# Winograd convolution on one core: the first input loads split by rows over two DMA queues, and zero-matmuls placed on both sides of the weight transposes

## The chip, the cores and the metric

The kernel runs on one core of one Trainium2 chip. The metric is the device time of one execution in microseconds (us); the time before is the median of three runs, 126.69 us (126.35 to 126.71). A core has five engines: TensorE (PE in the profile), VectorE (DVE), ScalarE (ACT), GpSimd (POOL) and SyncE (SP). SyncE, ScalarE and GpSimd can issue transfers; each of the three has a queue of its own, and the packets of all queues are carried by the same 16 DMA engines.

## The reference

A 3 x 3 convolution with padding 1, 16 images of 64 channels and 64 x 64 pixels, 128 output channels, all in float32:

```python
def setup_inputs():
    batch, c_in, h, w, c_out = 16, 64, 64, 64, 128
    ...
    x_pad = np.pad(x, ((0, 0), (0, 0), (1, 1), (1, 1)), mode='constant')
    ...
                        output[b, co] += weight[co, ci, kh, kw] * x_pad[b, ci, kh:kh+h, kw:kw+w]
```

The input has 16.8 MB, the output 33.6 MB, the weights 0.29 MB.

## The kernel before, in words

**Tiling.** Two images are one pair: their 2 x 64 channels fill the 128 partitions, one partition holding one channel's 64 x 64 pixels (16 KB). There are eight pairs (`p`), and a pair's 64 output rows are made in four blocks (`blk`) of 16 rows. A matmul uses the 64 partitions of one image and 512 columns (8 rows of 64); the matmuls of the two images stand in turn. Vertically the kernel computes two output rows from shared products (a small Winograd scheme): with `ss`, the sum of each even row and the odd row below it, it forms U = G1 * ss, then A from the odd rows (weights G2 - G1, and G0 on the row above) and B from the even rows (weights G0 - G1, and G2 on the row below). Even output rows are A + U, odd ones B + U. That is 30 matmuls a block, 120 a pair, 960 in all (L150). ScalarE copies U out of PSUM (L164), VectorE adds A and B to it (L174, L177) into `ots`, the two output tiles of the pair.

**The start, in program order.** SyncE issues the load of the weights `w_raw` (L42), then pair 0 as `x0` (L45) and pairs 1 to 3 as `xf` (L49), each one transfer of 2 MB in float32. VectorE clears `zeros` (L51). GpSimd makes an identity and casts the weights to float16 (`w16`, L61). TensorE transposes the weights by 18 matmuls against the identity (L93); ScalarE copies the three results to `Wt` (L94), ahead of which stands its table load. Then `spin(10)` runs ten matmuls of 512 columns on zeros (L56); they touch nothing that is used later. GpSimd makes the two differences of the weights (L96, L97) and issues the load of pair 4 (`load`, L67), which casts to float16 under way. VectorE makes the four row sums of pair 0 (L76 called from L100), and ScalarE casts pair 0 to float16 in the cuts 0 to 18, 18 to 34, 34 to 50 and 50 to 64 (L101).

**The main loop.** At the head of pair `p`, GpSimd makes the sums of pair `p + 1` in two instructions, for rows 0 to 31 and 32 to 63 (L76 called from L114), and, from pair 1 on, issues the load of pair `p + 4`. ScalarE casts pair `p + 1` while it is one of `xf`: rows 0 to 31 in block 2, rows 32 to 63 in block 3 (L169). At the end of a pair SyncE stores the first image's output; the second image's store waits in `held` and is issued by ScalarE in the next block after U was copied (L106 for both). The last pair is stored in halves, after block 1 and after block 3.

**Order.** The wrapper `keep` fixes an instruction's place in its engine's program order; waits on data are put in by the framework. A queue's transfers go in the order in which they were issued. The pool `opool` has eight tiles of 2 MB that `x0`, the three `xf` and all `ots` share in turn.

Of the kernel before, what the change touches and what calls it, by code (L numbers as in the profile page):

```python
# [8 lines left out]
F32 = mybir.dt.float32  # L9
# [4 lines left out]
def kernel(  # L14
# [6 lines left out]
    nc = tc.nc  # L21
    B, CI, H, W = x.shape
# [5 lines left out]
    keep = tc.keep_in_program_order  # L28
    x_rows = x.rearrange("b c h w -> (b c) h w")
# [6 lines left out]
    opool = ctx.enter_context(tc.tile_pool(name="opool", bufs=8))  # L36
# [5 lines left out]
    nc.sync.dma_start(w_raw, w_flat)  # L42
    x0 = opool.tile([128, H, W], F32, tag="ot", name="x0")
    cuts = [(0, 18), (18, 34), (34, 50), (50, 64)]
    nc.sync.dma_start(x0, x_rows[0:128, :, :])  # L45
    xf = {}
    for p in (1, 2, 3):
        xf[p] = opool.tile([128, H, W], F32, tag="ot", name="xf")
        nc.sync.dma_start(xf[p], x_rows[128 * p : 128 * p + 128, :, :])  # L49
    zeros = const.tile([128, 512], F16)  # L50
    keep(nc.vector.memset(zeros, 0.0))  # L51
    warm = psum.tile([128, 512], F32, tag="acc", name="warm")
# [1 line left out]
    def spin(n):  # L54
        for _ in range(n):
            keep(nc.tensor.matmul(warm, zeros[:, 0:128], zeros))  # L56

    ident = const.tile([128, 128], F16)
    make_identity(nc, ident)
    w16 = const.tile([CO, CI * 9], F16)  # L60
# [24 lines left out]
    def wrow(i):  # L85
        return Wt[:, i, :, :].rearrange("p t c -> p (t c)")

    for kh, g in ((1, G1), (2, G2), (0, G0)):
# [3 lines left out]
            for q in (0, 64):  # L92
                keep(nc.tensor.matmul(wp[q : q + 64, k * CO : k * CO + CO], w16[:, t::9], ident))  # L93
        keep(nc.scalar.copy(wrow(g), wp[:, 0 : 3 * CO]))  # L94
    spin(10)
    keep(nc.gpsimd.tensor_sub(wrow(G21), wrow(G2), wrow(G1)))  # L96
    keep(nc.gpsimd.tensor_sub(wrow(G01), wrow(G0), wrow(G1)))  # L97
    load(4)
# [12 lines left out]
    for p in range(NP):  # L111
# [8 lines left out]
        for blk in range(4):  # L120
# [58 lines left out]
            if blk in parts:  # L179
                lo, hi = parts[blk]  # L180
# [34 lines left out]
```

## Time and profile before

| | |
|---|---|
| median of the runs | 126.69 us |
| span of the profiled execution, first to last instruction | 124.8 us |
| TensorE busy | 108.2 us (87%) |
| VectorE, ScalarE, GpSimd busy | 82.8, 52.0, 36.2 us |
| bytes moved by the DMA engines | 46.57 MB, mean 373 GB/s |
| first matmul of the main loop starts | 9.92 us |
| last store issued | 113.95 us |

Only the span of the profiled execution is known; 126.69 - 124.8 = 1.9 us of the median lie outside it. The profile names a group of instructions by line, engine, operation and tiles. The GB/s of a transfer that casts count the float16 bytes written, half of the bytes read. The DMA share is the mean busy share of the 16 DMA engines in a stretch; a packet counts with the time it took, so a short stretch can show more than 1.

### The profile page before, as it was taken

How to read it: one execution, taken by the hardware profiler on the slowest of the kernel's cores; microseconds unless marked ns; L12 is line 12 of the kernel's file. 1: busy time of each engine (PE TensorE's matmuls, PEld its weight loads, DVE VectorE, ACT ScalarE, POOL GpSimd, SP SyncE). 2: the span in 40 equal slices, each digit the busy share in tenths (PEclk: the TensorE clock that was granted, in tenths of full speed). 3: DMA queues.
4: the chain of work that ended last, by engine and by line, in shares of the span. 5: the costliest groups of instructions: out<-in, count | busy, mean ns of one | idle time of the engine just before them, and what ended most of it. 6: DMA issues, size and time to landing. Idle time of an engine off the chain costs nothing.

```text
span 124.8 us, 2437 instructions
## 1 busy us (share of the span) xinstructions
PE 108.2 (87%) x988; PEld 49.3 (40%) x988; DVE 82.8 (66%) x133; ACT 52.0 (42%) x84; POOL 36.2 (29%) x27
## 2 busy tenths in 40 slices
PE   0699999999999999999999999999999999990000
PEld 0433444444444444444444444444444444440000
DVE  0016787878878787877777778777877787685000
ACT  4319749833993399333333333333333333330000
POOL 2360086294799202920067000940000000000000
PEclk9999999999999999999999999999999999999555
DMA  6899999999999999999999999999999999999991
GB/s 173 362 436 407 297 323 349 425 315 415 397 349 368 305 376 373 360 334 362 381 347 360 334 344 412 431 431 425 425 441 420 436 415 425 436 412 418 436 402 74
DMA packets 3898, 46.57 MB, mean 373 GB/s; under 512 B 432, under 2 KB 432, under 8 KB 560
## 3 DMA queue, kind: packets, MB, share of 16 engines
q1 hardware_dynamic: 2016, 25.46, 49.5%
q10 hardware_dynamic: 1296, 16.78, 31.6%
q0 software_dynamic: 576, 4.19, 16.1%
q8 instruction: 7, 0.11, 0.3%
q14 instruction: 3, 0.02, 0.0%
HBM read 17.07 MB, written 33.55 MB: 406 GB/s over the span
## 4 chain that ended last, share of the span: by engine, by line
PE 86%; DMA 2%; DVE 1%; issue 1%; POOL 1%; DVEq 0%
PE acc L150 81%; PE warm L56 4%; DMA w_raw<-in_weight_dram 2%; PE wp L93 1%; DVE ot L174 1%; POOL w L61 1%; DVE ot L177 0%; DVEq L210 0%; DVEq L174 0%
## 5 line engine op out<-in xcount | busy, mean ns | idle before, releaser
L150 PE MATMUL acc<-xs,Wt 64*128 64x504 f16 (+3 forms) x768 | 87.0, 373 | 0.0
L150 PEld LDWEIGHTS <-Wt 64*128 64x128 f16 x960 | 46.8, 94 | 56.2 <-issue 0.8
L164 ACT COPY ut<-acc 128x512 f32<-128x512 f32 x64 | 34.3, 588 | 52.9 <-issue 32.1
L174 DVE TENSOR_TENSOR ot<-acc,ut 128x512 f32<-128x512 f32 x64 | 41.2, 686 | 22.6 <-PE acc L150 18.3
L177 DVE TENSOR_TENSOR ot<-acc,ut 128x512 f32<-128x512 f32 x64 | 41.1, 684 | 0.0
L150 PE MATMUL acc<-ss,Wt 64*128 64x504 f16 (+1 forms) x192 | 26.0, 377 | 0.0
L76 POOL TENSOR_TENSOR ss<-xs 128x1024 f16<-128x1024 f16 x8 | 16.8, 2124 | 20.2 <-DMA xs<-in_x_dram 20.2
L76 POOL TENSOR_TENSOR ss<-xf 128x1024 f16<-128x1024 f32 x6 | 14.1, 2361 | 13.6 <-DMA xf<-in_x_dram 13.6
L169 ACT CAST xs<-xf 128x1024 f16<-128x1024 f32 x12 | 12.0, 1058 | 0.0
L76 DVE TENSOR_TENSOR ss<-x 128x512 f16<-128x512 f32 x4 | 2.5, 687 | 7.7 <-DMA x<-in_x_dram 7.7
L93 PE MATMUL wp<-ident,w 128*64 128x128 f16 x18 | 1.3, 328 | 4.3 <-POOL w L61 4.3
L101 ACT CAST xs<-x 128x1024 f16<-128x1024 f32 (+2 forms) x4 | 3.9, 1042 | 2.6 <-DMA x<-in_x_dram 2.6
L67 POOL DMA_DIRECT2D xs<-in_x_dram x4 | 2.4, 600 | 7.8 <-ACT xs L169 7.8
L56 PE MATMUL warm<-zeros 128*128 128x512 f16 x10 | 4.4, 631 | 0.0
L93 PEld LDWEIGHTS <-w 128*64 128x64 f16 x18 | 1.1, 210 | 4.3 <-POOL w L61 4.3
L94 ACT CAST Wt<-wp 128x384 f16<-128x384 f32 x3 | 1.2, 487 | 2.9 <-PE wp L93 2.9
L56 PEld LDWEIGHTS <-zeros 128*128 128x128 f16 x10 | 1.3, 143 | 2.3 <-issue 2.2
L94 ACT ACT_TABLE_LOAD x1 | 1.3, 1283 | 0.7 <-PEq L199 0.7
L96 POOL TENSOR_TENSOR Wt<-Wt 128x384 f16<-128x384 f16 x1 | 0.9, 907 | 1.7 <-ACT Wt L94 1.7
L61 POOL CAST w<-w_raw 128x576 f16<-128x576 f32 x1 | 0.7, 663 | 2.3 <-DMA w_raw<-in_weight_dram 2.3
L97 POOL TENSOR_TENSOR Wt<-Wt 128x384 f16<-128x384 f16 x1 | 0.9, 910 | 0.0
L51 DVE MEMSET zeros<- 128x256 uint32 x1 | 0.3, 272 | 0.9 <-PEq L199 0.9
(6 smaller groups left out, 0.9 us busy)
## 6 DMA issues: line engine op xcount, KB each, us to landing
out_dram<-ot SPq DMA_DIRECT2D x7, 2048.0 KB, 22.0
out_dram<-ot ACTq DMA_DIRECT2D x7, 2048.0 KB, 18.9
xf<-in_x_dram SPq DMA_DIRECT2D x3, 2048.0 KB, 22.1
xs<-in_x_dram POOLq DMA_DIRECT2D x4, 1024.0 KB, 23.4
x<-in_x_dram SPq DMA_DIRECT2D x1, 2048.0 KB, 7.6
out_dram<-ot SPq DMA_DIRECT2D x2, 1024.0 KB, 10.6
out_dram<-ot ACTq DMA_DIRECT2D x2, 1024.0 KB, 11.0
w_raw<-in_weight_dram SPq DMA_DIRECT2D x1, 288.0 KB, 2.8
```

Of the source, the lines that this page charges most:

```text
L56: keep(nc.tensor.matmul(warm, zeros[:, 0:128], zeros))
L61: keep(nc.gpsimd.tensor_copy(w16, w_raw))
L67: keep(nc.gpsimd.dma_start(xs[p], x_rows[128 * p : 128 * p + 128, :, :]))
L76: eng.tensor_add(ss[p][:, lo : lo + n, :], v[:, lo : lo + n, 0, :], v[:, lo : lo + n, 1, :])
L93: keep(nc.tensor.matmul(wp[q : q + 64, k * CO : k * CO + CO], w16[:, t::9], ident))
L94: keep(nc.scalar.copy(wrow(g), wp[:, 0 : 3 * CO]))
L101: keep(nc.scalar.copy(xs[0][:, lo:hi, :], x0[:, lo:hi, :]))
L150: nc.tensor.matmul(tiles[b2][:, lo - j0 : hi - j0, c_lo:c_hi], Wt[p0 : p0 + 64, wi, kw, :], rhs, start=i == 0, stop=i == n - 1,)
L164: keep(nc.scalar.copy(ut, U[b2]))
L169: keep(nc.scalar.copy(xs[q][:, lo : lo + 16, :], xf[q][:, lo : lo + 16, :]))
L174: nc.vector.tensor_add(ots[b2][:, j0 : j0 + RB, 0, :], A[b2], us[b2])
L177: nc.vector.tensor_add(ots[b2][:, j0 : j0 + RB, 1, :], Bt[b2], us[b2])
```

## The change

The loads of the first four pairs are cut by rows. Rows 0 to 31 of each pair are issued by SyncE, rows 32 to 63 by ScalarE, pair after pair, 1 MB each. `w_raw` stays on SyncE's queue ahead of them. Ten of the matmuls on zeros now stand ahead of the weight transposes, and six behind them, where ten stood before.

```diff
-    nc.sync.dma_start(x0, x_rows[0:128, :, :])
-    xf = {}
-    for p in (1, 2, 3):
-        xf[p] = opool.tile([128, H, W], F32, tag="ot", name="xf")
-        nc.sync.dma_start(xf[p], x_rows[128 * p : 128 * p + 128, :, :])
+    xf = {p: opool.tile([128, H, W], F32, tag="ot", name="xf") for p in (1, 2, 3)}
+    for p in range(4):
+        for eng, lo in ((nc.sync, 0), (nc.scalar, 32)):
+            keep(
+                eng.dma_start(
+                    xf.get(p, x0)[:, lo : lo + 32, :],
+                    x_rows[128 * p : 128 * p + 128, lo : lo + 32, :],
+                )
+            )
...
+    spin(10)
     ident = const.tile([128, 128], F16)
...
-    spin(10)
+    spin(6)
```

## The prediction

> **What bounds the kernel now.** I read the page's slices and queue table first, then the chain of waits, then windows at the start and where loads give way to stores, and last the timeline at both ends.
>
> ```profile
> DMA  6899999999999999999999999999999999999991
> q1 hardware_dynamic: 2016, 25.46, 49.5%
> q10 hardware_dynamic: 1296, 16.78, 31.6%
> q0 software_dynamic: 576, 4.19, 16.1%
> ```
>
> The three queues' packets fill 49.5 + 31.6 + 16.1 = 97.2% of 16 DMA engines' span, 121.3 of 124.8 us, and every slice between the ends shows 8 or 9. The chain of waits names another engine:
>
> ```profile
> 5.62 4.37 PE warm L56 x10
> 9.99 101.39 PE acc L150 x948
> 113.32 0.60 DVE ot L177
> ```
>
> TensorE runs without a hole for 101.39 us, but this chain ends with VectorE at 113.92, and the span at 124.8. What lies between is stores, as windows and timeline show (in a window's row the last two columns are the DMA share and the GB/s):
>
> ```profile
> 84.00:88.00 4.00, 4.00 (x40) 1.86 (x38) 3.27 (x6) 1.41 (x3) 0.00 (x0) 1.00 1.01 426
> 92.00:96.00 4.00, 4.00 (x42) 1.77 (x38) 3.13 (x6) 1.07 (x2) 0.00 (x0) 1.00 1.02 434
> 116.00:120.00 4.00, 0.00 (x0) 0.00 (x0) 0.00 (x0) 0.00 (x0) 0.00 (x0) 0.50 1.01 426
> ```
>
> ```profile
> 113.95 0.34 ACTq L106 DMA_DIRECT2D out_dram<-ot  x1
> ```
>
> A full DMA moves about 430 GB/s (the windows from 84 to 112 read 422 to 434), with rows of 16 KB as with the 8 KB rows of the last four stores (426). When the last store is issued at 113.95, DMA still has full work until 121 or 122. So DMA sets the end and TensorE is hidden; time can only come from moments in which DMA moves less than it could. There are two.
>
> ```profile
> 1.00:2.00 1.00, 0.00 (x0) 0.00 (x0) 0.13 (x1) 1.00 (x1) 0.29 (x1) 1.00 0.23 44
> 2.00:3.00 1.00, 0.00 (x0) 0.00 (x0) 0.00 (x0) 0.02 (x1) 0.00 (x0) 1.00 1.62 478
> 3.00:4.00 1.00, 0.00 (x0) 0.00 (x0) 0.00 (x0) 0.00 (x0) 0.41 (x1) 1.00 0.70 248
> 4.00:5.00 1.00, 0.69 (x12) 0.70 (x14) 0.00 (x0) 0.04 (x1) 0.25 (x1) 1.00 0.88 377
> ...
> 26.00:27.00 1.00, 1.00 (x14) 0.41 (x10) 1.00 (x3) 0.20 (x1) 1.00 (x2) 1.00 1.17 279
> 27.00:28.00 1.00, 1.00 (x12) 0.47 (x10) 0.39 (x1) 0.87 (x2) 1.00 (x1) 1.00 0.71 213
> 28.00:29.00 1.00, 1.00 (x14) 0.47 (x10) 0.89 (x2) 0.00 (x0) 1.00 (x2) 1.00 0.77 328
> ```
>
> The start: 44 KB at 430 GB/s is 0.1 us, so the first bytes come at 1.9. From there to 5.0 are 3.1 us, and 44 + 478 + 248 + 377 = 1147 KB are 2.67 us of work: 0.43 us is lost, between the small packets of `w_raw` and the first of `x0`. The handover: from 26 to 29, 820 KB move where 1290 could, and no casting load runs then whose bytes would count half; 470/430 = 1.1 us is lost.
>
> **The change, part by part.** It moves no byte less. SyncE still issues five transfers, its loads half as large; ScalarE issues four more.
>
> *The start of DMA.* Now 1.05 MB of pair 0 stands in ScalarE's queue from about 0.74 (where ScalarE's first instruction starts today), beside the 0.29 MB of `w_raw`: 1.34 MB, 3.1 us of work from 1.9 on, until 5.0. The gap between `w_raw` and `x0` is thereby filled. Bounds: 0 (the first packets of any queue are slow) to 0.43 us saved; I take 0.4, since each queue now has another beside it during its first packets. Smaller packets: the 426 of the 8 KB stores against 430 makes at most 1% of the loads' 19.5 us, 0.2 us; within the windows' scatter I take 0.
>
> *The handover.* No row tells why it dips. It falls between ScalarE's first use of its queue (a store issued at 24.30, SyncE's at 23.70) and the first stores' data. If the cause is ScalarE's queue being new, 1.1 us is saved, as that queue is now in use from the start; if it is the turn from loads to stores, nothing. Two queues turning at once could make it longer, by its own size at most. I take 0, the nearest reading, since the first stores still follow the loads.
>
> *ScalarE's issues.* Four of 0.34 to 0.42 us from 0.74 end by 2.4; the table load (1.28 us) would then end by 3.7, and the first copy of weights starts today at 4.96. That 1.2 us of cover hides it.
>
> *The weights.* `w_raw` lands at 3.53 today. Beside ScalarE's queue it comes later: if the queues share by bytes, by 0.29 MB/430 = 0.7 us, at 4.2; if packet takes turn with packet, each of an engine's 8 weight rows waits for one 8 KB packet (8.2 KB at 430/16 GB/s is 0.305 us), by 2.4 us, at 5.9. The rows from 12 to 16, where GpSimd's casting load runs beside `xf`, show about 300 GB/s: half of 430 plus a quarter, equal turns for equal packets. Unequal packets no row shows.
>
> *TensorE.* `zeros` is ready at 1.13; ten matmuls at today's spacing of 0.427 us (the weight loads of L56 at 5.95, 6.38, 6.81) end at 5.5. The transposes wait for the cast of the weights (landing + 0.06 + 0.67): they start at 5.5 to 6.6 instead of 4.30, and take 1.31. Six matmuls take 2.56 us at that spacing, or 1.3 at the 0.211 of the main loop (30 matmuls in 3.17 us, two images at a time). They end at 8.1 to 10.5. The second weight difference ends 3.4 us after the transposes start (4.30 to 7.68 today), at 8.9 to 10.0. *Pair 0's first half*: by bytes, 1.34 MB at half rate from 1.9 is at 8.15, and with today's lag (2.39 MB end at 7.9, gap included, landed 8.80) lands at 9.1; by turns, the weights end at 5.0 and eight turns of 0.61 us at 9.9, landing at 10.8. The first sum takes 0.69: the main loop starts at 9.8 to 11.5 against 9.92. I take 1 us later.
>
> *What covers it.* Two places. All loads up to pair 4 are 10.8 MB read, 25.1 us from 1.9: 27.0. The first store is issued at 23.70 and, by the 1.16 us from the issue of `w_raw` (0.74) to the first bytes, has data moving at 24.9: 2.1 us of cover. At the end the last two stores are 2.1 MB, 4.9 us; from an end near 122.3 their data starts at 117.4, while the last is issued at 113.95 and ready at 115.1: 2.3 us of cover. A main loop 1 us later costs nothing; one 1 us earlier would bring nothing.
>
> Sum: 0.4 us saved, the rest hidden: span 124.4, and with the 1.9 us outside it, 126.3; from the median, 126.69 - 0.4 = 126.3.
>
> **The rivals.**
>
> *The dip goes too.* For it: the dip comes 1.3 us after ScalarE's first use of its queue. Against it: GpSimd's queue, first used at 7.63, shows no such dip in the rows after. Time: 126.3 - 1.1 = 125.2.
>
> *The queues change nothing.* For it: the slices are full, and two queues move no more than one (5 to 10 averages 439, mostly SyncE's alone; 84 to 112 averages 430 with two). If the compiler puts ScalarE's table load first, its loads start 1.28 us later and miss most of the gap. Time: 126.7. [...]
>
> *DMA runs dry at the handover (slower).* The first stores come too late to follow the loads. Price: each us that the main loop starts later than 2.1 us (after 12.0) is a us of idle DMA. Turn-taking brings it to 11.5; if the matmuls on zeros end at 8.1, TensorE then idles 3.4 us, and after the last matmul (112.5) the clock column falls to 0.50 by 115.9, as long an idle time. 3.4 us at half speed lose 1.7, so that the first store comes 3.3 late: 1.2 us of dry DMA, 126.3 + 1.2 = 127.5. Against it: it needs turn-taking at its worst and the clock's fall. [...]
>
> **Chances.** Forecast 126.3: 0.42, split about evenly around the 0.3% (0.38 us) that a measurement of this kernel can tell from no change. The dip goes: 0.22. Nothing changes: 0.13. Dry DMA: 0.23. Faster 0.20 + 0.22 = 0.42, same 0.21 + 0.13 = 0.34, slower 0.24 with the forecast's upper edge. The forecast's own range is 125.9 to 126.7; with the dip gone at one end and the dry DMA at the other, the range is 125.1 to 127.5.
>
> **What would show it.** Right: windows from 2 to 5 at about 430 GB/s; `w_raw` landing after 4; the first L150 matmul at 9.8 to 11.5; L150 still without a hole; DMA share near 1 to the end, which comes 0.4 us earlier. Wrong: windows from 26 to 29 at 430 (the dip was the queue's), or emptier than now (dry DMA); a last store that lands at once after its issue, which would mean that TensorE sets the end; or a full rate other than 430 for the halved loads.

## The result, and the profile after

The change makes the kernel slower: 128.36 us (127.30 to 129.91) against 126.70 us (126.34 to 127.98), 16 runs each. The ratio is 1.011, 95% interval 1.008 to 1.014, or 1.4 us (1.1 to 1.7). Like the ratios of the experiments it is taken over the undisturbed runs alone (13 of the 16 here, 11 of 12 in e4, 9 of 13 in e6, whose profiled execution of 129.00 us is not among them, 5 of 6 in e10, all in the others); the medians take in all. The profiled execution has a span of 125.7 us against 124.8, so 0.9 us of the difference can be looked up in it; the rest of the 1.4 us cannot.

The page's slices and queues of the kernel after:

```profile
DMA  3999999999999999999999999999999979999991
...
q1 hardware_dynamic: 2016, 21.27, 40.6%
q10 hardware_dynamic: 1872, 20.97, 39.5%
```

4.2 MB have moved from SyncE's queue (q1) to ScalarE's (q10). Two slices are emptier than before: the first, and one near 103 us. The chain of waits of the kernel after (start us, us, what):

```profile
1.16 10.05 DMA x<-in_x_dram
...
11.24 0.70 DVE ss L81
...
11.98 101.56 PE acc L155 x919
```

The main loop starts at 11.98 instead of 9.92, and what it waits for is no longer the matmuls on zeros but pair 0's first half, which lands 10.05 us after its issue, at 11.21; whole `x0` had landed at 8.80. TensorE then runs as before, 101.56 us without a hole. The other half, rows 32 to 63, which is needed later, had landed long before. It was issued by ScalarE at 0.73, and the profile's page gives 6.8 us from issue to landing (last number), so it was there at 7.5:

```profile
x<-in_x_dram ACTq DMA_DIRECT2D x1, 1024.0 KB, 6.8
```

No run tries the halves the other way round. The timeline of the kernel after shows the weights late as well:

```profile
6.33 0.66 POOL L66 CAST w<-w_raw 128x576 f16<-128x576 f32 x1 [5.03 <-DMA w_raw<-in_weight_dram]
...
7.05 1.31 PE L98 MATMUL wp<-ident,w 128*64 128x128 f16 x18 [1.83 <-POOL w L66]
...
8.30 2.74 PE L60 MATMUL warm<-zeros 128*128 128x512 f16 x6
```

The cast of the weights starts at 6.33 where it started at 3.59, and the transposes at 7.05 instead of 4.30. The windows of the kernel after, at the places where the prediction looked and at one where it did not (last two columns: DMA share, GB/s):

```profile
1.00:2.00 1.00, 0.81 (x2) 0.28 (x3) 0.13 (x1) 0.00 (x0) 0.29 (x1) 1.00 0.35 18
2.00:3.00 1.00, 1.00 (x4) 0.43 (x3) 0.00 (x0) 0.00 (x0) 0.00 (x0) 1.00 0.50 67
3.00:4.00 1.00, 1.00 (x4) 0.33 (x3) 0.00 (x0) 0.99 (x1) 0.00 (x0) 1.00 1.04 407
...
26.00:29.00 3.00, 3.00 (x32) 1.62 (x30) 2.39 (x5) 0.90 (x3) 1.98 (x1) 1.00 1.06 448
...
102.00:104.00 2.00, 2.00 (x22) 1.08 (x20) 1.40 (x4) 1.07 (x2) 0.00 (x0) 1.00 0.55 229
```

The same window of the kernel before, 102 to 104:

```profile
102.00:104.00 2.00, 2.00 (x22) 0.88 (x18) 2.00 (x4) 0.36 (x1) 0.00 (x0) 1.00 1.02 434
```

Three things stand out. The start did not get fuller but emptier: 85 KB from 1 to 3 us against 522. The dip from 26 to 29 is gone (448 against a mean of 273). And from 102 to 104 DMA moves at 229 GB/s where it had moved at 434: (434 - 229) x 2/430 = 0.95 us of work is missing. The store of pair 6 shows why, by ScalarE's issues, before and after:

```profile
101.14 0.34 ACTq L106 DMA_DIRECT2D out_dram<-ot  x1
```

```profile
103.34 0.34 ACTq L111 DMA_DIRECT2D out_dram<-ot  x1
```

It comes 2.2 us later, and by then the queues have next to nothing left.

### The profile page after: what moved, and what is told of

Same layout as the page of the kernel before. It is cut to its first block, busy times and chain, and to the rows that moved or that the text cites. A ratio compares the mean times of both kernels' runs of the same rounds, so it can differ in the third digit from the quotient of the medians.

```text
span 125.7 us, 2454 instructions
## 1 busy us (share of the span) xinstructions
PE 111.0 (88%) x994; PEld 57.7 (46%) x994; DVE 82.7 (66%) x133; ACT 51.9 (41%) x84; POOL 36.2 (29%) x27
## 4 chain that ended last, share of the span: by engine, by line
PE 81%; DMA 8%; DVE 2%; issue 1%; DVEq 0%; SPq 0%
PE acc L155 81%; DMA x<-in_x_dram 8%; DVE ot L179 1%; DVE ss L81 1%; DVE ot L182 0%; DVEq L215 0%; SPq L42 0%; DVEq L179 0%
## 5 line engine op out<-in xcount | busy, mean ns | idle before, releaser
L155 PE MATMUL acc<-xs,Wt 64*128 64x504 f16 (+3 forms) x768 | 93.1, 373 | 0.0
L155 PEld LDWEIGHTS <-Wt 64*128 64x128 f16 x960 | 54.5, 94 | 49.9 <-issue 2.1
L155 PE MATMUL acc<-ss,Wt 64*128 64x504 f16 (+1 forms) x192 | 31.8, 377 | 0.9 <-DVE ss L81 0.9
L81 POOL TENSOR_TENSOR ss<-xs 128x1024 f16<-128x1024 f16 x8 | 16.8, 2128 | 19.2 <-PE acc L155 10.8
L60 PE MATMUL warm<-zeros 128*128 128x512 f16 x16 | 6.8, 602 | 1.2 <-DVE zeros L55 1.2
L60 PEld LDWEIGHTS <-zeros 128*128 128x128 f16 x16 | 2.1, 141 | 4.6 <-issue 3.3
## 6 DMA issues: line engine op xcount, KB each, us to landing
out_dram<-ot SPq DMA_DIRECT2D x7, 2048.0 KB, 17.7
xs<-in_x_dram POOLq DMA_DIRECT2D x4, 1024.0 KB, 22.9
```

The lines of the kernel that those rows point to most:

```text
L81: eng.tensor_add(ss[p][:, lo : lo + n, :], v[:, lo : lo + n, 0, :], v[:, lo : lo + n, 1, :])
L155: nc.tensor.matmul(tiles[b2][:, lo - j0 : hi - j0, c_lo:c_hi], Wt[p0 : p0 + 64, wi, kw, :], rhs, start=i == 0, stop=i == n - 1,)
```

## The experiments

Theory A: the second queue delays the weights and pair 0's first half; the main loop starts 2 us late; the stores come late, and DMA runs dry. Rival B: the split transfers themselves cost the time. Rival C: the moved matmuls and TensorE's clock do. All times below are ratios to the kernel before, taken on the same chip, with a 95% interval.

**The matmuls on zeros alone** (e1): the loads as before.

```diff
+    spin(10)
     ident = const.tile([128, 128], F16)
...
-    spin(10)
+    spin(6)
```

> Only the matmuls on zeros are changed (ten ahead of the transposes, six behind); the loads are those of the kernel before. Theory A (the split loads bring the weights and pair 0's first half later, so the main loop starts 2 us later, the stores come later and DMA runs dry between the stores of two pairs): weights land near 3.5, x0 near 8.8, the main loop starts at 9.5 to 9.9, time within 0.3% of 126.7. Rival C (the moved matmuls and the TensorE clock cost the time): a main loop that starts after 10.5 or runs slower than 101.4 us, and 1% more time.

Measured: 0.999 (0.997 to 1.001). The chain of waits of this run shows the main loop at 9.63, behind the first sum:

```profile
8.86 0.02 issue
8.89 0.70 DVE ss L77
...
9.63 101.56 PE acc L151 x919
```

Rival C falls. And a main loop 0.3 us earlier brings nothing that can be measured, as the prediction held.

**The loads alone** (e2): the split loads, with ten matmuls on zeros behind the transposes as before.

```diff
-        nc.sync.dma_start(xf[p], x_rows[128 * p : 128 * p + 128, :, :])
...
+        for eng, lo in ((nc.sync, 0), (nc.scalar, 32)):
...
     spin(10)
```

> Only the loads are changed (halves on two queues); ten matmuls on zeros behind the transposes as before. Theory A: pair 0's first half lands near 11.2, main loop near 12, time about 1.1% more than before, like the whole change. Rival B (what costs is not the late main loop but the split transfers as such: lower rate, slower first bytes): about 1.1% as well. Rival C: 126.7.

Measured: 1.008 (1.005 to 1.011). Chain and window of this run:

```profile
1.17 9.88 DMA x<-in_x_dram
...
11.82 101.56 PE acc L154 x919
```

```profile
102.00:104.00 2.00, 2.00 (x22) 1.09 (x20) 1.40 (x3) 1.07 (x2) 0.00 (x0) 1.00 0.56 238
```

The same late half, the same late main loop, the same dry window. The cost sits in the loads; A and B stand.

**A late main loop alone** (e3): no transfer is touched.

```diff
-    spin(10)
+    spin(20)
```

> The kernel before with twenty instead of ten matmuls on zeros, the loads untouched: the main loop is pushed from 9.9 to about 12.0 (ten more at 0.21 us, or up to 14 if they run at 0.43). Theory A: the same dry windows between the stores of two pairs, near 40 to 44 and 102 to 104, and about 1% more time though no transfer was changed. Rival B: 126.7, since the last two stores have 2.3 us of cover.

Measured: 1.009 (1.006 to 1.012). The chain and the window of this run:

```profile
5.74 6.28 PE warm L56 x20
12.02 101.39 PE acc L150 x948
```

```profile
102.00:104.00 2.00, 2.00 (x22) 0.97 (x20) 1.42 (x3) 1.07 (x2) 0.00 (x0) 1.00 0.44 188
```

With the loads of before, 2.0 us of delay (12.02 against 9.99) give the dry window and 1.15 us of time (0.91% of 126.6). Most of the change's cost is the late main loop.

**Halves on one queue** (e4): the whole change, but ScalarE's part goes back to SyncE.

```diff
-        for eng, lo in ((nc.sync, 0), (nc.scalar, 32)):
+        for eng, lo in ((nc.sync, 0), (nc.sync, 32)):
```

> The whole change, but both halves are issued by SyncE, so the second queue is not used for loads. Theory A: weights land near 3.5 and pair 0's first half near 6.5, the main loop starts at 8.5 to 9.5 behind the matmuls on zeros, no dry windows, time 126.0 to 126.7. Rival B in the form that halved transfers move slower: 1% more than before in spite of the early start. If DMA alone set the end, as the prediction had it, 126.7.

Measured: 1.003 (1.001 to 1.006). The timeline of TensorE in this run:

```profile
7.77 0.82 PE L155 MATMUL acc<-ss,Wt 64*128 64x512 f16 x6
...
12.23 1.96 PE L155 MATMUL acc<-xs,Wt 64*128 64x512 f16 x13 [0.48 <-ACT ut L169]
```

Pair 0's first half landed at 6.4 and the main loop started at 7.77, 2.2 us earlier than in the kernel before. The hole at 12.23 stands behind ScalarE's copies of U, which had to follow its casts of the second half, landed at 8.85. So with halves on one queue the first half is not late (6.4 against 11.21 in the change); the second queue makes it so. The early start brought no time at all: 0.3% was lost, which A did not foresee. Most of the lead was gone before the end: pair 0's first store is issued at 22.48 against 23.70, but ScalarE's store of pair 6 at 100.86 against 101.14, because VectorE had to wait 2.2 us for a store to empty an output tile (columns: us in all, times, longest):

```profile
DVE ot L179 <- DMA out_dram<-ot: 2.2, 1, 2.2
```

TensorE waited for it in turn, until 66.18. e9 comes back to the 0.3%.

**Four us late** (e7), and **one us late** (e6): `spin(30)` and `spin(15)` instead of `spin(10)`, nothing else.

> Fifteen matmuls on zeros instead of ten, loads untouched: the main loop starts near 11.0, one us late. Theory A with a cover of about 1.1 us ahead of the last pair's store: no dry window, at most 0.3% more time. Without any cover (each us late is a us more): 0.8% more.

Measured: 0.999 (0.997 to 1.002). Five more matmuls take 1.1 to 2.1 us by the spacings of 0.21 and 0.43, so by this reckoning a delay of at least 1.1 us is free; no trace shows it. The run's only trace is of that execution of 129.00 us. Its main loop starts at 11.36, 1.4 us late, and its DMA is short of full from 100 to 104 (295 and 328 GB/s in two windows).

> Thirty matmuls on zeros, loads untouched: the main loop starts near 14.1, twice as late as with twenty. Theory A: past the cover every us of a late main loop is a us of dry DMA, so 2.1 us more than with twenty, near 130.1, with the dry window ahead of the last pair's store near 3 us of lost work. If the loss with twenty had another cause than the late stores, the time would not follow at one us per us.

Measured: 1.022 (1.018 to 1.026), 2.8 us. In the profiled execution the main loop started at 13.04, earlier than expected: its matmuls on zeros went over from 0.43 to 0.21 us apart at 7.2, where e3's did at 9.5. The window ahead of pair 6's store:

```profile
102.00:105.00 3.00, 3.00 (x34) 1.44 (x30) 2.42 (x5) 1.07 (x2) 0.00 (x0) 1.00 0.45 191
```

(430 - 191) x 3/430 = 1.7 us of missing work, against 1.1 with twenty (188 for two us). The time grows with the delay, as A says, from 1.15 us (2.0 us late) to 2.8 (3.1 us late). The windows show it only weakly: e3's DMA was already short from 100 to 102 (328 GB/s, 0.5 us more), so that it misses 1.6 us in all. The size per us is not exact, because the start differs from run to run.

**The second queue, issued later** (e8): pair 0 whole on SyncE's queue, the second halves of pairs 1 to 3 on ScalarE's, behind its copies of the weights; the matmuls on zeros stand as in the change.

```diff
+    keep(nc.sync.dma_start(x0, x_rows[0:128, :, :]))
...
+    for p in (1, 2, 3):
+        half(nc.sync, p, 0)
...
+    for p in (1, 2, 3):
+        half(nc.scalar, p, 32)
+    spin(6)
```

> Two queues without the turn-taking at the start: pair 0 whole on SyncE's queue behind the weights, first halves of pairs 1 to 3 behind it, second halves on ScalarE's queue but issued behind its copies of the transposed weights. Theory A: weights land near 3.5, x0 at 8.8 to 9.4, main loop at 9.6 to 10.2, no dry window ahead of the last pair's store, 126.5 to 127.0. Rival B (splitting the loads over two queues costs as such): near the time of the whole change, 1% more. It also shows whether the dip from 26 to 29 stays when ScalarE's queue is not new but loads stand in both queues as the first stores are issued.

Measured: 1.0035 (1.001 to 1.006); x0 landed at 8.71, the main loop started at 9.45, and the window at pair 6's stores is full:

```profile
102.00:104.00 2.00, 2.00 (x22) 1.08 (x20) 1.89 (x4) 0.69 (x2) 0.00 (x0) 1.00 1.00 426
```

Two queues with halves are 0.8% faster than in the change if only they don't compete in the first microseconds. B as the main cause falls. But again 0.3% remains.

**Four more transfers** (e9): the kernel before with four loads of 4 KB into tiles that nothing reads.

```diff
+    for i in range(4):
+        touch = const.tile([128, 64], F32, name=f"touch{i}")
+        keep(nc.scalar.dma_start(touch[0:16, :], w_flat[0:16, 64 * i : 64 * i + 64]))
```

> The kernel before with four small loads (4 KB each, into tiles that nothing reads) on ScalarE's queue at the start, so that it has as many transfers as the whole change. Theory T (besides the late main loop, the four more transfers shift which of SyncE's closing waits is the last store's: it is then waited for with six more waits of about 61 ns behind it, where the kernel before has two): the last data as before, but 0.25 to 0.35 us more from there to the end, time 0.1 to 0.4% more. Rival H (the halved rows themselves move slower, which made the two runs with halves and no late main loop 0.33 and 0.35% slower): 126.7, no change.

Measured: 1.0026 (1.0007 to 1.005). At the end SyncE waits for the outstanding semaphores one after the other, some 61 ns each. Before, one more wait stands behind the last store's; with four more transfers the semaphores are dealt out in another order, the last store's is asked for early, and in the change five more are walked behind it, four more than before: 4 x 61 ns. SyncE's waits for stores at the end, before and after (us in all, times, longest), show the other order: before it comes to a store that is still under way five times, in the change only twice, the two last stores, and all the rest of the list stands behind them.

```profile
SPq L210 <- DMA out_dram<-ot: 9.9, 5, 3.6
```

```profile
SPq L215 <- DMA out_dram<-ot: 8.6, 2, 7.8
```

From the last landing in the trace to the end are 0.96 us in the kernels before, e1 and e3; 1.20 in the change, e2 and e9; 1.28 and 1.27 in e4 and e8. So T holds, with 0.24 us where 0.25 to 0.35 was expected, and it can be the remainder in e4 and e8: their 0.33 and 0.35% lie within the interval of e9. That H adds nothing is not shown, only that it is not needed.

**The change with four more transfers** (e10): the same four loads added to the whole change.

> The whole change with the same four small loads, which shift the closing waits by four more. Theory T: the last store's wait comes late again, 0.2 to 0.3 us less than the whole change, near 0.8% more than the kernel before. Rival H: no less than the whole change, 1.1% more than before.

Measured: 1.078 (1.073 to 1.082), a miss. The walk at the end is 0.96 us again, as T says, but the chain of waits shows something else:

```profile
1.65 14.53 DMA xf<-in_x_dram
...
16.20 0.32 ACTq L56
16.52 0.03 issue
16.55 1.28 ACT L102
```

The small loads waited on ScalarE until earlier transfers had landed, at 16.18, and with them the table load and the copies of the weights behind them; the main loop started at 20.19. The expectation had given these issues no cost and had overlooked their wait.

**The first touch of ScalarE's queue** (e5): the kernel before with one load of 32 KB there at the start.

> The kernel before with one small load (32 KB) on ScalarE's queue at the start, into a tile that nothing reads. It asks what the dip of DMA from 26 to 29 is, which the whole change no longer shows. If the queue's first use makes it: windows from 26 to 29 near 430 GB/s, and 0.5 to 0.7% less time than before. If stores that begin while loads still stand in the queues make it: the dip stays, 126.7.

Measured: 1.002 (0.999 to 1.006). The window of this run:

```profile
26.00:29.00 3.00, 3.00 (x31) 1.58 (x29) 2.27 (x5) 1.07 (x2) 3.00 (x2) 1.00 0.98 289
```

The dip stays, so it is not the queue's first use.

**The first stores later** (e11): both stores of pair 0 by ScalarE, one block later.

```diff
-            while held:
+            while held and (p, blk) != (1, 0):
...
+                if p == 0:
+                    held.append((p, 0, ots[0], lo, hi))
+                else:
+                    store(nc.sync, p, 0, ots[0], lo, hi)
```

> The kernel before, but both stores of pair 0 are issued by ScalarE one block later, near 27.4 instead of 23.7 and 24.3. It asks for the cause of the dip from 26 to 29. If stores that begin while loads stand in the queues make it, and it does not move with them: windows from 26 to 29 near 430 GB/s, 0.5 to 1 us less time than before, faster than both kernels. If DMA then runs dry instead, because the loads end near 27: a hole of about 1 us there and 126.7. If the dip belongs to the loads or to the clock time: it stays where it is, 126.7.

Measured: 1.011 (1.007 to 1.016). Two windows of this run, the second of which reads 371 GB/s in the kernel before:

```profile
26.00:29.00 3.00, 3.00 (x31) 1.58 (x29) 2.27 (x5) 1.07 (x2) 3.00 (x2) 1.00 0.92 388
32.00:36.00 4.00, 4.00 (x40) 2.14 (x38) 3.27 (x6) 3.72 (x5) 3.98 (x4) 1.00 1.03 320
```

The dip is mostly gone from 26 to 29, so it goes with the first stores and not with the loads; but of the 0.8 us that DMA gains there against the kernel before it loses 0.5 again from 32 to 36 (part of it may be the casting load of pair 5, whose bytes count half), and the kernel is slower. Why it is 1.1% slower no run shows. In e8 the dip is there too (341), with loads in both queues. DMA is not idle in it: in the kernel before, packets of 16 KB that start from 26 to 28 take up to 1.7 us where 0.61 is usual, and in e11 packets from 33 to 35 take up to 1.2. What makes them slow stays open, and no version here beat the kernel before.

**Whole pairs on two queues** (e12): as many transfers as before, packets of 16 KB.

```diff
-        nc.sync.dma_start(xf[p], x_rows[128 * p : 128 * p + 128, :, :])
+        eng = nc.sync if p == 2 else nc.scalar
+        keep(eng.dma_start(xf[p], x_rows[128 * p : 128 * p + 128, :, :]))
```

> The kernel before, whole pairs, but pairs 1 and 3 are issued by ScalarE, 0 and 2 by SyncE: as many transfers as before, packets of 16 KB beside the small ones of the weights. It asks how two queues share the DMA engines. If packet takes turn with packet: each of an engine's 8 weight packets waits for one of 0.61 us (16 KB at 430/16 GB/s), so the weights land near 8, then x0's 8 packets take 1.22 us each and it lands at 17.5 to 18.5; the main loop starts at 18.2 to 19.2, 8 to 9 us late, and past the cover of 1 to 2 us the time is 132.5 to 135. If they share by bytes: weights by 6.3 at the latest, as in the whole change, x0 near 13.5, main loop near 14.2, time 129 to 130.

Measured: 1.083 (1.079 to 1.088). The timeline of this run:

```profile
8.95 0.66 POOL L62 CAST w<-w_raw 128x576 f16<-128x576 f32 x1 [7.65 <-DMA w_raw<-in_weight_dram]
...
19.86 1.29 DVE L77 TENSOR_TENSOR ss<-x 128x512 f16<-128x512 f32 x2 [18.73 <-DMA x<-in_x_dram]
```

The weights landed at 8.9 and x0 at 19.8. With 8 KB beside them the weights had landed at 6.3, alone at 3.5: in these three runs the delay goes with the size of the other queue's packets. Sharing by bytes, reckoned at 6.3 and 13.5, does not fit; turns of packet with packet do, somewhat worse than their reckoning of 8 and 18. The packet records of the change count the same way: from 3.5 to 5.0 us, 60 rows of the weights (2.3 KB) start on SyncE's queue and 59 rows of 8 KB on ScalarE's. Here DMA ran dry at the handover, 26 GB/s from 28 to 36, the place that the prediction's rival had named.

## Why the prediction was wrong

**DMA is the bound.** Right for the kernel before: a main loop 0.3 us earlier (e1) brought nothing, and one 2.2 us earlier (e4) lost most of its lead on the way, part of it to a wait for a store. It is no longer so after the change.

**What covers a late main loop: two places, 2.1 and 2.3 us.** This is the step that failed. It looked at the handover and at the last two stores, and not at the stores in between. After 76 us there are only stores; a pair makes 4.2 MB in 12.8 us, 330 GB/s, and DMA carries 430, so each pair eats some 3 us of the backlog, and it is thinnest when pair 6's stores come. The traces give the cover there. In four runs in which DMA had run dry, the last data follow ScalarE's store of pair 6 by the same time, though that store is 2.0 to 12.9 us late in them: the last landing is 21.2 us behind it in the change (103.34 to 124.53), in e2 (103.18 to 124.42), in e10 (111.53 to 132.72) and in e12 (114.05 to 135.25). In the kernel before it is 22.7 (101.14 to 123.82). So by this count the cover was 1.5 us, not 2.1 or 2.3. Of the 2.2 us that the store is late in the change, 0.7 reach the last landing; with the 0.24 us of closing waits (e9) they are the 0.9 us of the two spans.

The count depends on the last packets, which trail by a time that varies: e3's and e7's last landings follow by 22.9 and 22.2. Up to the point where 1 MB is left to move, the distance is 18.1 and 18.0 in these two, 17.7 to 17.8 in the other four, and 18.9 in the kernel before, a cover of 0.8 to 1.2. The cover was therefore between 0.8 and 1.5 us.

**The main loop 1 us later.** The sum took 1 of the bounds 9.8 to 11.5; it came at 11.98, behind turn-taking at its worst and a landing at 11.21 instead of 10.8. Of the two ways of sharing, the second is the one that e12 fits (weights at 8.9, x0 at 19.8); taking the middle was the mis-sized term. It took both errors to miss: 1 us late would have cost 0.2 us at most by the cover above, and 2.06 us late nothing by a cover of 2.1.

**0.4 us saved at the start.** Wrong in sign: by 10 us the windows have moved 3.07 MB against 3.34, 0.6 us less work. ScalarE's queue was issued at 0.73, but its first packet starts at 3.0, and full rate comes only then (67 KB from 2 to 3, 407 from 3 to 4), as in e2 (95 and 439). Why two queues start more slowly together was not tried. By the fixed 21.2 us behind pair 6's store this loss did not add to the time, nor did the 1.2 us won at the handover (448 against 273 over 3 us) come off it: what DMA gains or loses ahead of a dry stretch vanishes in that stretch. This is reckoned from the fixed distance; no run changes that loss or gain alone.

**Smaller packets at nothing, ScalarE's issues hidden.** Right: no run needs a cost for the 8 KB rows, and the table load (3.01 to 4.29) was out of the way before the copies. What was missing is the closing list of waits, 0.24 us in the change, 0.26% in e9.

**The rivals.** The slower one had the right mechanism, dry DMA behind a late main loop, with a chance of 0.23, but its place was wrong for a delay of 2 us, and so its price: a main loop at 11.98 lies within its 12.0 and would have cost nothing. *The dip goes too* named something that happened, but the queue's first use was not the reason (e5), and it saved no time; 430 GB/s from 26 to 29 was not the sign that the prediction took it for. The slower rival's 1.2 us and the 127.5 also count on 3.4 us at half speed, a length that no row of the kernel before shows. The trace of the change does: the clock column stands at 0.50 from 8.1 to 11.5. But that ends before the main loop starts at 11.98, so it fell on the six matmuls on zeros (2.74 us) and not on the main loop, whose first six take 0.82 us as before. *The queues change nothing* held for the rate: from 4 to 10 us DMA moved 429 GB/s with one queue and 430 with two. What decided was the order.

The sum that holds: 0.91% for the late main loop (e3) and 0.26% for the closing waits (e9) make 1.17%, against 1.11% (0.83 to 1.38) measured; each of the two has an interval of its own (0.6 to 1.2 and 0.07 to 0.46), so the agreement is closer than they warrant.

## What to carry to other kernels

Here a second queue added no bandwidth to a full DMA (430 GB/s from 4 to 10 us, against 429) but reordered it: the small load of the weights, needed first, landed at 6.3 beside the other queue's packets of 8 KB and at 8.9 beside packets of 16 KB, where it had landed at 3.5 alone. So transfers that nobody waited for yet were better issued behind those that were needed first: e8 was 0.8% faster than the change. The cover of a late stage is the smallest backlog at any later point (here 0.8 to 1.5 us, at pair 6's stores), not that at the end; where transfers come in bursts, reckon it for each burst. Past that point the time grew with the delay (1.15 us for 2.0 us late, 2.8 us for 3.1); that gains of DMA ahead of it are lost is reckoned and not shown by a run.

## What was not expected of the hardware

TensorE's clock fell in the change after a pause of only 1.8 us. The ten matmuls end at 5.2 and the transposes start at 7.05, yet the clock column reads 0.5 in the next microseconds:

```profile
8.00:9.00 1.00, 1.00 (x8) 0.46 (x7) 0.00 (x0) 0.90 (x3) 0.40 (x1) 0.54 1.02 434
9.00:10.00 1.00, 1.00 (x4) 0.32 (x3) 0.00 (x0) 0.00 (x0) 1.00 (x2) 0.50 1.04 442
```

The six matmuls behind the transposes took 2.74 us there, but 1.47 in e1 and e4, where the weights came in time. (The column alone would not show it: it reads 1.00 also from 5.6 to 9.9 in the kernel before, where matmuls go 0.43 us apart.) The prediction had read 3.4 us from the end of the kernel before. By the trace the last matmul ends there at 112.55 and the column falls at 115.66, 3.1 us later; in the change these are 114.94 and 117.31, 2.4 us. So the runs show no single idle time ahead of the fall, and at the start of the change it came behind a pause of 1.8 us. Nor does the pause's length alone decide: in e1 TensorE paused for 2.0 us ahead of the main loop, but the column stays at 1.00 (the mean of the span is 0.969 against 0.953 in the change), and the next six matmuls take 0.82 us, as in the kernel before.

```profile
9.63 0.82 PE L151 MATMUL acc<-ss,Wt 64*128 64x512 f16 x6 [1.99 <-DVE ss L77]
```

What decides stays open.
